# First layer of a two-layer decoder trunk: normalising after the first projection instead of before it

## The chip, the cores and the metric

The kernel runs on one core of a Trainium2 chip. The metric is the device time of one execution in microseconds. The core has a tensor engine (PE, with its weight loads shown as PEld), a vector engine (DVE), a scalar engine (ACT), GpSimd (POOL), and a sync engine (SP) that issues nearly all DMAs. Each engine works off its own queue of instructions and waits at semaphores for the others.

## The reference, cut to what matters

Two layers act on x of 512 rows by 1024 columns, in float32:

```
h = RMSNorm(x) * norm_g              # rstd by row, gain by column
p = h @ w_in                         # 1024 -> 3488 columns
cq, ckv, kr, g_a, c_h, c_b, c_c, g_b, sg_u, sg_v, g_c, mq, mk, mv, g_d = split(p)
o_a = latent attention: q = rmsnorm(rmsnorm(cq) @ w_uq), k and v from rmsnorm(ckv) @ w_ukv, rotary part
o_b = c_b * causal_conv3(c_c * c_h)
o_c = sg_u * (masked 128x128 mix of layernorm(sg_v))
o_d = block attention with q = rmsnorm(mq), k = rmsnorm(mk), v = mv
x   = x + concat(o_a silu(g_a), o_b silu(g_b), o_c silu(g_c), o_d silu(g_d)) @ w_out
```

Since rstd is one number per row of x, p of a row is that number times the row of (x * norm_g) @ w_in. Where p goes into another RMSNorm or LayerNorm, the factor cancels but for the epsilon, which has to be divided by rstd squared, that is, multiplied by the mean square.

## The kernel before, in words

**Precision.** Every matrix is kept as a high part in the fast float32 format of the tensor engine and a low part (the remainder). A product is three matmuls: high by high, high by low, low by high (mm3). High parts are made by a copy on ACT or DVE (split2, split_units), low parts by a subtraction on DVE or POOL (low_half).

**Order of the work.** The order of each engine's instructions is written out by a planner in Python: every step of the kernel is a generator (a "chain") that asks an engine for an instruction with an estimated cost and resumes when the planned clock has come that far. What a chain issues stands in the engine's queue from then on; the queues are worked off in that order on the chip. All instructions of the chains are recorded at one line of a helper (L164 for ACT, DVE and POOL, L194 for PE, L273 for most DMAs), so the profile is read by tile names. A chain made with a later start time (its due time) is recorded later. DMAs on SP are recorded at the moment the planner reaches them, if a buffer is free; the planner assumes that they land some microseconds on.

**The first layer's start.** start() (L1548) loads x in four row tiles of 128x1024 and the weights c0 to c3 of the first projection (416 columns: cq, ckv, kr; two of the eight contraction blocks in each unit). For each row tile square_half (L628) sums the squares on ACT, pre_norm (L632) makes rstd on POOL (xss), multiplies x by rstd and norm_g on DVE (h), transposes it on PE (hT) and splits it (hTh on ACT, hTl on DVE). norm_g is spread to all partitions by two PE matmuls (ng). Warm-up matmuls (warm) that compute nothing fill PE until about 15 us of planned time. The main generator (L1357) then goes through the row tiles one after the other: tok (L1360) runs all eight contraction blocks of one row tile into one accumulator bank (cq). As soon as a row tile is done, low_chain (L717) multiplies by the gains (ct), transposes (cT) and runs the second projections (q, kv).

**What follows.** Units of weights are loaded through two raw buffers (rawS; four early ones through others) and split; three accumulator banks (accS), three banks for scores (sS) and two for transposes (trS) are handed from step to step. After cq come the sq block (sg_v and mq, four row tiles of 24 matmuls), ga0, ga1, the kv block (mk, mv), and the features su0 to gc1, each 24 matmuls of 512 columns; the attention heads run between them. mix_chain (L837) loads and masks the mixing weights (sgw), and issues the mix products (mp) on PE. rope_tables (L481) makes the sine and cosine tables by polynomials, about 60 small operations on rope_scratch that go to DVE or to POOL, whichever the planner finds free, with a pause from 4.7 to 15.5 us.

**Parameters.** load_params (L565) loads the gains and biases with thirteen small DMAs, most of them spread to all partitions (cg_b, gq_b, gk_b, gr_b, lg_b, lb_b, dq_b, dk_b, ...), when the unit ukv has been issued. In it scale() (L586) multiplies gq_b and dq_b by constants on POOL, in layer 0 not before the planned time MIXT = 23 us:

```
        def scale():
            ch = Chain(o, L.par_t)
            yield from ch.pool(G.tensor_scalar, L.gq, L.gq, -(96 ** -0.5), None, op0=ALU.mult)
            yield from ch.pool(G.tensor_scalar, L.dq, L.dq, -0.125, None, op0=ALU.mult)
        o.spawn(scale(), None if L.l else MIXT, 2)
```

**End of a layer.** The output projection is one Strassen step (seven products of half size, banks oz, ox, oy, line L1382), after which the second layer runs the same code, with its rows normalised before the projection.

Of the kernel before, what the change touches and what calls it, by code (L numbers as in the profile page):

```python
# [11 lines left out]
F32 = mybir.dt.float32  # L12
# [26 lines left out]
ROPEB, ROPEV = 400.0, 200.0  # L39
# [113 lines left out]
class Chain:  # L153
    def __init__(self, o, t=None):
        self.o = o
        self.t = o.now if t is None else t
        self.pe_t = None

    def _emit(self, e, cost, f, a, k):
        while self.t > self.o.now + SLACK:  # L160
            yield self.t - SLACK
        self.o.clk[e] = max(self.o.clk[e], self.t, self.o.now) + cost
        self.t = self.o.clk[e] + LAT
        f(*a, **k)  # L164
# [19 lines left out]
    def pe(self, cost, f, *a, **k):  # L184
# [3 lines left out]
        if self.o.now < self.o.fill_until:  # L188
            for _ in range(int((self.o.now - self.o.pe_end) * FILL / 110.0)):
                self.o.fill()  # L190
# [16 lines left out]
def hybrid_trunk(ctx: ExitStack, tc: tile.TileContext, x, positions, norm_g, w_c, w_f, w_t, w_o, mla_q_norm_g,  # L207
# [33 lines left out]
    zzS = Slots(o, 1, lambda name: wk.tile([P, S + 2], F32, tag="zz", name=name))  # L241
# [37 lines left out]
    class Unit:  # L279
        def __init__(self, src, a, b, name):  # L280
            self.src, self.a, self.b, self.name = src, a, b, name
            self.loaded, self.ready, self.wanted = Event(), Event(), False
            self.half, self.landed = [Event(), Event()], [Event(), Event()]
            self.slots = eS if name[:-2] in EARLY else wS
# [84 lines left out]
    def load_units():  # L369
        for u in order:  # L370
            ch = Chain(o)
            u.raw_slots = rawS
            if u.name in ("c2_0", "c3_0") or u.name[:-3] in ZPROD and u.name[-3] == "1":
# [8 lines left out]
            if u.name == "c0_0":  # L382
                for i in range(2):
# [3 lines left out]
                    o.set(u.landed[i], ch.t)  # L387
            else:
# [6 lines left out]
    def split_units(i0, i1):  # L395
        for u in order[i0:i1]:
# [5 lines left out]
            for i in range(2):  # L402
# [9 lines left out]
                if o.clk["V"] + 600.0 < o.clk["A"] and u.idx > 3:  # L412
# [3 lines left out]
                if u.idx < 4:  # L416
                    o.spawn(low_half(u, i, c2, lo, raw, hi), None, LOPRIO)
# [8 lines left out]
    def low_half(u, i, ch, lo, raw, hi):  # L426
        if (u.name, i) in LOPOOL:
# [29 lines left out]
    nhalf = cst.tile([P, 16], F32, name="nhalf")  # L457
# [15 lines left out]
    posf = cst.tile([P, NT], F32, name="posf")  # L473
    inv = cst.tile([P, 16], F32, name="inv")
    nc.scalar.dma_start(junk[0:NT, 0:P].bitcast(I32), dram(positions, 0, [[P, NT], [1, P]]))
    G.tensor_copy(junk[0:NT, P:2 * P], junk[0:NT, 0:P].bitcast(I32))
# [4 lines left out]
    def rope_tables():  # L481
# [9 lines left out]
        def free_engine():  # L491

            while True:
                if ch.t > o.now + SLACK:
                    yield ch.t - SLACK
                if PAUSE[0] < o.now < PAUSE[1]:
                    yield PAUSE[1]
                if o.clk["V"] <= o.now + ROPEV:
                    return True
                if o.clk["G"] <= o.now + SLACK:  # L500
                    return False
                yield o.now + 60.0

        def dv(f, *a, **k):
            if (yield from free_engine()):
# [4 lines left out]
        def stt(out, in0, c, in1, op0, op1):  # L510
            if (yield from free_engine()):
# [53 lines left out]
    def load_params(L):  # L565
# [24 lines left out]
        o.spawn(scale(), None if L.l else MIXT, 2)  # L590

    layers = []
    for l in range(DEPTH):
# [4 lines left out]
        L.xss = [cst.tile([P, 4], F32, name=f"xss{t}_{l}") for t in range(NT)]  # L598
# [12 lines left out]
        L.hT_free, L.p1, L.h_done, L.h = Event(), Event(), [Event(), Event()], {}  # L611
        L.s = {n: [Event() for _ in range(4)] for n in ("t2", "t1", "b22")}
# [11 lines left out]
    def pow_rstd(ch, dst, src, n):  # L624
        return ch.pow(G.tensor_tensor, dst, src, nhalf[:, :n], op=ALU.pow)

# [62 lines left out]


    def low_stats(L, t, a, t0, done):
# [9 lines left out]
        yield from ch.dve(V.tensor_scalar, m[:, 0:2], ssq[:, t, 1:3], 1.0, EPS, op0=ALU.mult, op1=ALU.add)  # L701
        yield from ch.dve(V.tensor_scalar, m[:, 2:4], ssq[:, t, 0:2], EPS, EPS * EPS, op0=ALU.mult, op1=ALU.add)
# [14 lines left out]
    def low_chain(L, t, a, t0):  # L717
        ch = Chain(o, max(t0, L.par_t))
        l = L.l
        done = shared(accS, 2)  # L720
# [30 lines left out]
    def q_chain(L, t, q_ps, t0):  # L751
# [13 lines left out]
        for h in range(4):  # L765
            yield from ch.act(A.activation, junk[:, :96], Q[:, t, h, :], AF.Square, accum_out=m[:, h:h + 1])
# [3 lines left out]
        yield from pow_rstd(ch, m[:, 4:8], m[:, 0:4], 4)  # L770
        for h in range(4):
# [8 lines left out]
    def kv_chain(L, t, kv_ps, t0):  # L780
# [22 lines left out]
        for h in range(4):  # L803
            yield from ch.act(A.activation, junk[:, :64], K[:, t, h, 0:64], AF.Square, accum_out=m[:, h:h + 1])
# [8 lines left out]
    def sv_chain(L, t, a, t0, put):  # L813
# [11 lines left out]
        yield from ch.pool(G.tensor_scalar, mv[:, 1:2], mv[:, 1:2], 1.0, EPS, op0=ALU.mult, op1=ALU.add)  # L825
# [11 lines left out]
    def mix_chain(L):  # L837
# [32 lines left out]
    def gate(ch, a, name):  # L870
        th = yield from t2S.get(ch, f"th_{name}")
        yield from ch.act(A.activation, th, a, AF.Tanh, scale=0.5)
# [55 lines left out]

    def su_chain(j):
        def f(L, a, t0):  # L930
# [3 lines left out]
            accS.put(ch)  # L934
            yield from ch.wait(L.mix_ev)
# [6 lines left out]
            yield from ch.dve(V.tensor_tensor, u, mt, u, op=ALU.mult)  # L942
# [5 lines left out]
    def finish(ch, L, kt, yv, tg):  # L948
        yield from ch.dve(V.scalar_tensor_tensor, yv, in0=yv, scalar=0.5, in1=tg, op0=ALU.mult, op1=ALU.mult)
# [14 lines left out]
    def ch_chain(j):  # L964
        def f(L, a, t0):
# [3 lines left out]
            accS.put(ch)  # L969
            o.set(L.b_ev[j][0], ch.t)  # L970
        return f

    def cc_chain(j):
        def f(L, a, t0):
# [5 lines left out]
            yield from ch.dve(V.tensor_tensor, zz[:, 2:S + 2], a, c, op=ALU.mult)  # L980
# [5 lines left out]
            zzS.put(ch)  # L986
            o.set(L.b_ev[j][1], ch.t)
        return f

    def cb_chain(j):  # L990
        def f(L, a, t0):
            ch = Chain(o, t0)
            yield from ch.wait(L.b_ev[j][1])
            yield from ch.dve(V.tensor_tensor, L.b[j], a, L.b[j], op=ALU.mult)
# [22 lines left out]
    def mqk_chain(nm):  # L1017
        def f(L, t, a, t0, put):
# [12 lines left out]
            for h in range(4):  # L1031
                yield from ch.act(A.activation, junk[:, :64], dst[:, t, h, :], AF.Square, accum_out=m[:, h:h + 1])
            yield from ch.pool(G.tensor_scalar, m[:, 0:4], m[:, 0:4], 1.0 / 64, EPS, op0=ALU.mult, op1=ALU.add)
            yield from pow_rstd(ch, m[:, 4:8], m[:, 0:4], 4)
            for h in range(4):
# [10 lines left out]
    def mv_chain(L, t, a, t0, put):  # L1046
# [6 lines left out]
        yield from split2(ch, mt[:, :, 0:64], mt[:, :, 64:128], a[:, 0:256].rearrange("p (h d) -> p h d", h=4))  # L1053
# [51 lines left out]
    def pv_chain(L, H):  # L1105
# [25 lines left out]
        if h == 3:  # L1131
            v4S.put(ch)
            v4S.put(ch)
        H.ya_left[0] -= 1
# [222 lines left out]
    def main():  # L1357
        m = Chain(o)

        def tok(L, n, width, t, dst, us):  # L1360

            for k in range(KT):
# [3 lines left out]
                if (n, t, L.l) == ("c", 0, 0):  # L1366
                    us[k // 2:] = [(yield from unit(m, f"{n}{k // 2}_{L.l}", k % 2))]
                elif len(us) == k // 2:
# [7 lines left out]
                yield o.now  # L1376

# [4 lines left out]
        def seven(L):  # L1382
# [36 lines left out]
            slot = {"z0": accS, "z1": accS, "x0": accS, "x1": sS, "y0": sS, "y1": sS}  # L1419
            for n in ZPROD:  # L1420
                for i in range(2):
                    b = home.get(n, "y") + str(i)
                    ev = evs[n, i] = Event()
                    if n in ("b11", "t3"):
# [4 lines left out]
                    if (l, n, i) == (DEPTH - 1, "b22", 1):  # L1429
                        ev2 = Event()  # L1430
                        yield from z_out(L, "u", i, a, m.t, ev2, sS.put)
# [6 lines left out]
                    if n == "b11":  # L1438
                        y = bank[f"y{i}"] = yield from sS.get(m, f"oy{i}_{l}")
# [12 lines left out]
        for L in layers:  # L1452
# [8 lines left out]
            for t in L.torder:  # L1461
                a = yield from accS.get(m, f"cq{t}_{l}")
                yield from tok(L, "c", 416, t, a[:, 0:416], us)
                o.spawn(low_chain(L, t, a, o.now + PELAT))
# [7 lines left out]
            for n in SEQ:  # L1472
                if n in TOKS:
                    us = []
                    for t in range(NT):
                        a = yield from accS.get(m, f"{n}{t}_{l}")
# [189 lines left out]
```

## Time and profile before

| what | value |
|---|---|
| median of 3 runs | 499.86 us (498.12 to 500.18) |
| the profiled execution's own time | 499.26 us |
| its span | 497.6 us |
| PE busy | 490.7 us, 99% |
| DVE, ACT, POOL busy | 384.1 (77%), 320.7 (64%), 150.6 us (30%) |
| DMA | 81.98 MB, mean 165 GB/s |

A row of the timeline reads: start in us, duration in us, engine, line, operation, output tile <- input tiles, shapes, count, and in brackets how long the engine sat idle before it and who released it. A row of a group reads: busy us, mean ns of one | idle us before it and what ended that. A row of a window reads: stretch, its length, busy us (and instructions) of PE, PEld, DVE, ACT and POOL, granted clock, DMA share, GB/s. A row of DMA issues ends with the size of one and the median us from issue to landing. Matmul durations overlap, since matmuls are pipelined: the distance from start to start says what one costs. SPq is SP's issuing of DMAs.

### The profile page before, as it was taken

How to read it: one execution, taken by the hardware profiler on the slowest of the kernel's cores; microseconds unless marked ns; L12 is line 12 of the kernel's file. 1: busy time of each engine (PE TensorE's matmuls, PEld its weight loads, DVE VectorE, ACT ScalarE, POOL GpSimd, SP SyncE). 2: the span in 40 equal slices, each digit the busy share in tenths (PEclk: the TensorE clock that was granted, in tenths of full speed). 3: DMA queues.
4: the chain of work that ended last, by engine and by line, in shares of the span. 5: the costliest groups of instructions: out<-in, count | busy, mean ns of one | idle time of the engine just before them, and what ended most of it. 6: DMA issues, size and time to landing. Idle time of an engine off the chain costs nothing.

```text
span 497.6 us, 7823 instructions
## 1 busy us (share of the span) xinstructions
PE 490.7 (99%) x2459; PEld 416.4 (84%) x2459; DVE 384.1 (77%) x998; ACT 320.7 (64%) x938; POOL 150.6 (30%) x310
## 2 busy tenths in 40 slices
PE   8999989999999999999999999999999999999997
PEld 5998878888888888888889987788888888888886
DVE  3887885567797978699898698757888979765992
ACT  5788754557767786667566995557868676524640
POOL 4656785566100000000041478634250010000000
PEclk9999999999999999999999999999999999999999
DMA  8446549472752445587573232576259464475652
GB/s 306 110 144 212 198 100 235 147 156 54 202 139 84 149 148 135 157 315 247 165 258 129 84 125 88 193 191 102 67 191 232 150 154 122 166 258 180 229 171 96
DMA packets 35459, 81.98 MB, mean 165 GB/s; under 512 B 7125, under 2 KB 16857, under 8 KB 35162
## 3 DMA queue, kind: packets, MB, share of 16 engines
q1 hardware_dynamic: 26960, 73.09, 43.1%
q0 software_dynamic: 8448, 8.39, 11.3%
q8 instruction: 19, 0.31, 0.3%
q14 instruction: 22, 0.18, 0.1%
q10 hardware_dynamic: 10, 0.01, 0.0%
HBM read 73.61 MB, written 24.64 MB: 197 GB/s over the span
## 4 chain that ended last, share of the span: by engine, by line
PE 89%; DVE 3%; ACT 3%; POOL 3%; issue 1%; POOLq 0%; DVEq 0%
PE kv L194 10%; PE cq L194 8%; PE oy L194 6%; PE ch L194 4%; PE cc L194 4%; PE gd L194 4%; PE gb L194 4%; PE cb L194 4%; PE gc L194 4%; PE su L194 4%; PE ox L194 4%; PE oz L194 4%; PE sa L194 3%; PE ga L194 2%; PE od L194 2%; PE oa L194 2%
## 5 line engine op out<-in xcount | busy, mean ns | idle before, releaser
L164 ACT ACTIVATE pd<-pd,mnd 128x256 f32<-128x256 f32 (+3 forms) x48 | 26.0, 555 | 1.4 <-DVE mnd L164 1.4
L164 ACT ACTIVATE pha<-pTa 128x512 fp32r<-128x512 f32 (+3 forms) x32 | 13.9, 436 | 20.0 <-PE pTa L194 19.8
L194 PE MATMUL kv<-whi_kv,hTh 128*128 128x512 f32 x64 | 25.9, 405 | 0.0
L164 ACT ACTIVATE pa<-pa,mna 128x256 f32<-128x256 f32 (+3 forms) x46 | 23.9, 537 | 2.7 <-DVE mna L164 2.7
L164 ACT ACTIVATE phd<-pTd 128x512 fp32r<-128x512 f32 (+3 forms) x32 | 13.8, 434 | 17.8 <-PE pTd L194 17.8
L164 DVE TENSOR_TENSOR pla<-pTa,pha 128x512 fp32r<-128x512 f32 (+3 forms) x32 | 15.2, 484 | 12.8 <-ACT pha L164 12.7
L194 PE MATMUL kv<-whi_kv,hTl 128*128 128x512 f32 x64 | 25.0, 391 | 0.0
L194 PE MATMUL kv<-wlo_kv,hTh 128*128 128x512 f32 x64 | 24.9, 390 | 0.0
L194 PE MATMUL cq<-whi_c,hTh 128*128 128x416 f32 x64 | 24.4, 382 | 0.0
L339 POOL DMA_DIRECT2D t<-in_w_o_dram x16 | 17.5, 1097 | 19.9 <-DMA t<-t 19.3
L194 PE MATMUL cq<-whi_c,hTl 128*128 128x416 f32 x64 | 23.0, 360 | 0.0
L194 PE MATMUL cq<-wlo_c,hTh 128*128 128x416 f32 x64 | 22.9, 357 | 0.0
L164 POOL TENSOR_SCALAR xss<-xss 128x1 f32<-128x1 f32 x8 | 3.1, 391 | 61.8 <-ACT jk L164 49.1
L164 ACT ACTIVATE whi_t<-raw_t 128x512 fp32r<-128x512 f32 x31 | 18.2, 621 | 5.7 <-DMA raw_t<-t 5.7
L164 DVE TENSOR_TENSOR wlo_t<-raw_t,whi_t 128x512 fp32r<-128x512 f32 x32 | 21.1, 683 | 0.0
L164 DVE CUSTOM_DVE_ANT_0 pa<-sa,maskb 128x512 f32<-128x512 f32 (+3 forms) x32 | 15.0, 482 | 6.2 <-PE sa L194 3.1
L164 DVE CUSTOM_DVE_ANT_0 pd<-sd,maskb 128x256 f32<-128x256 f32 (+3 forms) x32 | 14.9, 485 | 5.9 <-PE pTd L194 2.8
L194 PE MATMUL sq<-yTh,hTh 128*128 128x512 f32 x48 | 18.9, 393 | 0.0
L194 PE MATMUL sq<-yTh,hTl 128*128 128x512 f32 x48 | 18.7, 390 | 0.0
L194 PE MATMUL sq<-yTl,hTh 128*128 128x512 f32 x48 | 18.7, 389 | 0.0
L164 DVE TENSOR_TENSOR pld<-pTd,phd 128x512 fp32r<-128x512 f32 (+3 forms) x32 | 15.3, 482 | 3.2 <-ACT phd L164 3.1
L164 ACT ACTIVATE whi_b<-raw_b 128x512 fp32r<-128x512 f32 x24 | 14.5, 622 | 4.2 <-DMA raw_b<-in_w_o_dram 4.2
(379 smaller groups left out, 1856.0 us busy)
## 6 DMA issues: line engine op xcount, KB each, us to landing
t<-in_w_o_dram POOLq DMA_DIRECT2D x16, 512.0 KB, 6.7
raw_t<-t SPq DMA_DIRECT2D x16, 512.0 KB, 4.2
raw_b<-in_w_o_dram SPq DMA_DIRECT2D x12, 512.0 KB, 4.4
raw_sq<-in_w_t_dram SPq DMA_DIRECT2D x8, 512.0 KB, 3.6
t<-in_w_o_dram SPq DMA_DIRECT2D x8, 512.0 KB, 4.4
raw_kv<-in_w_t_dram SPq DMA_DIRECT2D x8, 512.0 KB, 3.5
t<-t SPq DMA_DIRECT2D x8, 512.0 KB, 5.5
ys<-ysc SPq DMA_DIRECT2D x14, 256.0 KB, 4.8
```

What stands on the lines that cost most here:

```text
L164: f(*a, **k)
L194: f(*a, **k)
L339: nc.gpsimd.dma_start(z_src(l, n, j), quad(l, b, j), accum_op=ALU.add, max_dma_last_dim=1024)
```

## The change

In layer 0 the rows are no longer normalised ahead of the projection.

- x is loaded by column blocks (two of 128 columns, then three of 256, for all 512 rows), interleaved with the units c0 to c3. Each block of 128 columns is transposed on PE as it is (xT); norm_g, now a column per block (gcol), is applied in the split (x_parts).
- c_first runs the first projection with the contraction outside: for each column block the 12 products of the four row tiles, in the order high by high, low weights, low x. Four banks (three accS, one sS) are open at once. The last two blocks go by row tile. The low halves of c0 both, and the first halves of c1 to c3, are made on POOL; the high parts on DVE.
- x_stats sums the squares of x in 16 pieces on ACT; rstd (r) and the scaled epsilons are made for all rows at once. They are applied to results: in v of the block attention, in the gates (a DVE multiply by the row rh, half of rstd spread over partitions by two PE matmuls, x_row), and on POOL in by_rstd for su, ch and the convolution.
- head_sums may square on POOL and add on DVE instead of four squares on ACT, in both layers.
- The rope table starts on DVE (five operations) and goes on on POOL, without the pause.
- scale() has no due time of its own any more; users of gq_b and dq_b wait for it in the plan (g_ev). uq and ukv are loaded through the two h buffers, so that they and the parameters need not wait for a raw buffer.
- mix_chain of layer 0 is due at 42 us instead of 23, and in both layers its products are issued 2 us after the last row it needs.
- In the Strassen step the banks change places (z1 and x0 in sS, y0 and y1 in accS), and the bank x1 is taken when the last head of the block attention is done.
- Fill matmuls are fewer and different.

```diff
-NWARM, FILL, FILLEND = 3, 0.6, 15000.0
-ROPET, PAUSE, MIXT = 3900.0, (4700.0, 15500.0), 23000.0
-LOPOOL = (("c0_0", 1), ("c1_0", 1), ("c2_0", 1), ("c3_0", 1))
+NWARM, FILL, FILLEND = 4, 0.7, 15000.0
+MIXT, MIXLAG, ROWT = 42000.0, 2000.0, 38000.0
+KSPLIT, SQPOOL, LOVEC = 6, 200.0, 1
...
-            if u.name in ("c2_0", "c3_0") or u.name[:-3] in ZPROD and u.name[-3] == "1":
+            if u.name in ("uq_0", "ukv_0"):
+                u.raw_slots = hS
+                u.raw = yield from hS.get(ch, f"raw_{u.name}")
+            elif u.name in ("c2_0", "c3_0") or u.name[:-3] in ZPROD and u.name[-3] == "1":
...
-        if (u.name, i) in LOPOOL:
+        if i == 0 or u.idx < LOVEC:
             yield from ch.pool(G.tensor_tensor, lo, raw, hi.bitcast(F32), op=ALU.subtract)
...
             yield from ch.pool(G.tensor_scalar, L.dq, L.dq, -0.125, None, op0=ALU.mult)
-        o.spawn(scale(), None if L.l else MIXT, 2)
+            o.set(L.g_ev, ch.t)
+        o.spawn(scale(), None, 2)
...
+    def x_parts(k, tp, t0):
+        L, ch = layers[0], Chain(o, t0)
...
+        yield from ch.act(A.activation, hi, tp, AF.Copy, scale=g)
+        o.set(xhi[k], ch.t)
+        yield from ch.dve(V.scalar_tensor_tensor, lo, in0=tp, scalar=g, in1=hi.bitcast(F32),
+                          op0=ALU.mult, op1=ALU.subtract)
...
+        yield max(o.now, ch.t) + MIXLAG
         L.mix = (yield from hS.get(ch, f"mix{l}")).rearrange("p (n g d) -> p n g d", n=NT, g=4)
...
+        if name[-1] == "0":
+            yield from ch.wait(rh_ev)
+            yield from ch.dve(V.tensor_tensor, th, a, rh_box[0][:, 0:S], op=ALU.mult)
...
+            yield from x_transpose(0)
+            for k in range(KSPLIT):
+                for i in range(3):
+                    yield from ready(k, i)
+                    for t in range(NT):
+                        yield from part(k, t, i)
+                    if i == 0 or i == 1 and k + 1 == KSPLIT:
+                        yield from x_transpose(k + 1 + i)
...
-            slot = {"z0": accS, "z1": accS, "x0": accS, "x1": sS, "y0": sS, "y1": sS}
+            slot = {"z0": accS, "z1": sS, "x0": sS, "x1": sS, "y0": accS, "y1": accS}
...
+                    if b == "x1":
+                        yield from m.wait(L.s_done)
```

More of the change, by code (lines that the diff above doesn't have):

```diff
@@ L282, in __init__ @@
             self.loaded, self.ready, self.wanted = Event(), Event(), False
-            self.half, self.landed = [Event(), Event()], [Event(), Event()]
+            self.half, self.high, self.landed = ([Event(), Event()] for _ in range(3))
             self.slots = eS if name[:-2] in EARLY else wS
@@ L770, in q_chain @@
         yield from pow_rstd(ch, m[:, 4:8], m[:, 0:4], 4)
+        yield from ch.wait(L.g_ev)
         for h in range(4):
@@ L927, in s_chain, with by_rstd @@
         o.set(L.s["b22"][kk], ch.t)
+    def by_rstd(ch, z, n):
+        yield from ch.wait(rh_ev)
+        for _ in range(n):
+            yield from ch.pool(G.tensor_tensor, z, z, rh_box[0][:, 0:S], op=ALU.mult)
+        rh_put(ch)
     def su_chain(j):
@@ L1545, in hybrid_trunk @@
     L0 = layers[0]
-    L0.x0, L0.xh = [Event() for _ in range(NT)], [Event(), Event()]
     def start():
```

332 lines of the change are left out of this document (232 added, 100 removed).

## The prediction

> **What bounds the kernel now.** I read the page first (busy shares, chain), then the waits of the tensor engine (PE), then its timeline at the start, then the windows around its few gaps.
>
> ```profile
> span 497.6 us, 7823 instructions
> PE 490.7 (99%) x2459; PEld 416.4 (84%) x2459; DVE 384.1 (77%) x998; ACT 320.7 (64%) x938; POOL 150.6 (30%) x310
> PE 89%; DVE 3%; ACT 3%; POOL 3%; issue 1%; POOLq 0%; DVEq 0%
> ...
> PE mp L194 <- ACT vnh L164: 2.1, 2, 1.3
> ...
> 69.00:71.00 2.00, 0.69 (x4) 0.27 (x2) 1.90 (x5) 1.76 (x8) 1.39 (x3) 1.00 0.99 151
> 71.00:73.00 2.00, 1.89 (x11) 1.52 (x12) 1.06 (x6) 0.78 (x2) 1.92 (x2) 1.00 1.12 195
> 310.00:320.00 10.00, 9.12 (x45) 7.32 (x44) 6.92 (x21) 5.49 (x15) 6.24 (x18) 1.00 0.56 210
> ```
>
> PE is the bound from end to end. The only gaps behind the start and ahead of the tail are those at the spatial mix (mp), where PE waits for the split rows vn: 1.31 + 0.11 + 0.88 = 2.3 us not busy in these three windows. Neither PE's useful instructions nor their shapes change, so the change is worth what it does to the start and to gaps. The start:
>
> ```profile
> 1.26 2.93 PE L1557 MATMUL warm<-ones 128*128 128x256 f32 x6 [1.26 <-DVE ones L164]
> 9.90 1.06 PE L194 MATMUL hT<-ident,h 128*128 128x128 f32 x4
> 10.62 0.69 PE L194 MATMUL cq<-whi_c,hTh 128*128 128x416 f32 x1
> ...
> 12.57 0.55 PE L194 MATMUL cq<-wlo_c,hTh 128*128 128x416 f32 x1
> 12.92 0.55 PE L194 MATMUL cq<-whi_c,hTl 128*128 128x416 f32 x1
> ...
> 13.98 0.43 PE L194 MATMUL cq<-whi_c,hTh 128*128 128x416 f32 x1
> ...
> 14.63 0.35 PE L194 MATMUL cq<-whi_c,hTh 128*128 128x416 f32 x1
> 14.82 0.35 PE L194 MATMUL cq<-wlo_c,hTh 128*128 128x416 f32 x1
> ...
> 16.20 0.60 PE L194 MATMUL hT<-ident,h 128*128 128x128 f32 x4
> 16.55 0.44 PE L194 MATMUL cq<-whi_c,hTh 128*128 128x416 f32 x1
> ```
>
> Most of the 14 us is warm-up (fill) matmuls, which compute nothing. A cq matmul starts every 0.35 us at 12.6 us and every 0.19 us from 14.6 us on; four transposes take 0.35. By 13.98 us PE has done six cq matmuls and eight transposes, 6 x 0.19 + 2 x 0.35 = 1.84 us of full-speed work: the start loses 13.98 - 1.84 = **12.1 us**. That is the sum's reference.
>
> **The start after the change.** Column block 0 of x and the first half of c0 are enough for the first products, so on paper PE starts early. But the order of instructions of the changed program shows what stands in the way. GpSimd (POOL) now has, ahead of everything of the projection: the scaling of gq_b, the scaling of dq_b, then both low halves of c0 (wlo_c), then the rope table. Before, the two scalings came after all low halves and all four rstd. They moved because scale() is no longer held to 23 us, and the parameter loads, no longer kept back by a raw slot, are recorded at once, so that the planned landing lies at 4 us. On PE the ninth product (wlo_c of column block 0) is queued right behind eight transposes and four cq matmuls. So: dq_b lands -> POOL scales it -> POOL makes wlo_c -> PE goes on. Whether POOL really stands behind such a load, and what the steps cost:
>
> ```profile
> 6.91 1.06 POOL L164 TENSOR_TENSOR wlo_c<-raw_c,whi_c 128x416 fp32r<-128x416 f32 x1 [0.50 <-ACT whi_c L164]
> ...
> 24.67 0.46 POOL L164 TENSOR_SCALAR gq_b<-gq_b 128x96 f32<-128x96 f32 x1
> 25.21 0.37 POOL L164 TENSOR_SCALAR dq_b<-dq_b 128x64 f32<-128x64 f32 x1
> ...
> 196.24 0.47 POOL L164 TENSOR_SCALAR gq_b<-gq_b 128x96 f32<-128x96 f32 x1 [22.16 <-DMA gq_b<-in_mla_q_g_dram]
> 199.04 0.37 POOL L164 TENSOR_SCALAR dq_b<-dq_b 128x64 f32<-128x64 f32 x1 [2.33 <-DMA dq_b<-in_moba_q_g_dram]
> ```
>
> In layer 1 POOL sits idle for gq_b and then again for dq_b, in its order; there nothing urgent is queued behind. In layer 0 of the changed kernel wlo_c is.
>
> When does dq_b land? It is the eighth of the parameter loads in SP's queue, and in the listing each load waits for the one eight places ahead of it: dq_b for raw_ukv, which is behind all of x, c and raw_uq.
>
> ```profile
> 12.00:13.00 1.00, 1.00 (x5) 0.95 (x5) 1.00 (x3) 1.00 (x4) 0.63 (x2) 1.00 1.00 404
> 13.00:14.00 1.00, 1.00 (x8) 0.88 (x6) 1.00 (x2) 1.00 (x3) 1.00 (x2) 1.00 0.42 166
> ...
> 13.81 0.33 SPq L273 DMA_DIRECT2D raw_ukv<-in_mla_w_ukv_dram  x1
> 17.51 0.43 SPq L550 DMA_DIRECT2D dq_b<-in_moba_q_g_dram  x1
> 195.19 0.33 SPq L550 DMA_DIRECT2D dq_b<-in_moba_q_g_dram  x1
> ...
> raw_uq<-in_mla_w_uq_dram SPq DMA_DIRECT2D x1, 384.0 KB, 6.2
> raw_ukv<-in_mla_w_ukv_dram SPq DMA_DIRECT2D x1, 256.0 KB, 2.7
> dq_b<-in_moba_q_g_dram SPq DMA_DIRECT2D x1, 32.0 KB, 5.7
> ```
>
> Before, x, c and raw_uq (4 MB) keep the queue full until about 13.4 us (404 GB/s, then 166 in the window in which they end). Changed, raw_ukv's 262 kB follow without a pause: 262/404 = 0.65 us, so 14.1, landing at about 14.4 us. dq_b is then issued at 14.5. From issue to landing it took 5.7 us at the start of before; in layer 1, 199.04 - 195.19 = 3.85 us; a quiet load like raw_ukv 2.7 us. From raw_ukv's landing (13.81 + 2.7 = 16.5) to dq_b's (23.2) it was 6.7 us. That bounds dq_b's landing to 17.1 (14.4 + 2.7) and 21.1 us (14.4 + 6.7); I take 14.5 + 5.7 = **20.2 us**, its own row with the same small loads ahead of it. x now comes in runs of 512 bytes and 1 KB, for which no row gives a rate; the 0.9 us up to the upper bound have to cover a slower x.
>
> Then 0.37 for dq_b, 1.06 for wlo_c, 0.2 for the hand-overs (24.67 + 0.46 to 25.21 is 0.08 each): PE goes on at 21.8 us. It has by then done four cq matmuls and eight transposes, 1.46 us. After more than ten idle microseconds I take it to start at the slow spacing: from 10.62 to 13.98 us it cost 3.36 x (1 - 0.19/0.35) = 1.5 us; bounds are 0 and half of the whole slow stretch of before (1.26 to 13.98), some 5.8 us; I take 1.5, measured on the same matmuls. Loss 21.8 - 1.46 + 1.5 = 21.9 us, against 12.1: **+9.8 us**. The Trainium skill (TensorE: Matmul & The Clock Gate, What's actually happening) has the array at half clock by default, at full after a window of about 3.4 us of activity, and back at half after one idle window. The profile's granted clock says 1.00 throughout, while the spacing halves at 13.98, so the spacing decides; by that page an unlucky window would cost up to 3.4 us (6.8 us at half rate) instead of 1.5, and the sum would be 1.9 us higher.
>
> **The other parts, each against its cover.** The second wlo_c of c0 stands behind five rope operations and itself costs 1.06 to 1.28; POOL needs 3.3 us for them, PE has twelve slow products, 4.2 us, so no wait; the later low halves have longer.
>
> ```profile
> L164 POOL TENSOR_SCALAR rope_scratch<-rope_scratch 128x64 f32<-128x64 f32 x23 | 10.2, 443 | 2.2 <-DVE rope_scratch L164 0.9
> L164 POOL TENSOR_TENSOR rope_scratch<-rope_scratch 128x64 f32<-128x64 f32 x11 | 6.1, 555 | 0.9
> L164 POOL TENSOR_TENSOR wlo_c<-raw_c,whi_c 128x416 fp32r<-128x416 f32 x4 | 5.1, 1284 | 0.9 <-ACT whi_c L164 0.9
> L164 POOL TENSOR_TENSOR mq<-mq,nhalf 128x4 f32<-128x4 f32 x4 | 4.1, 1036 | 7.8 <-DVE mq L164 4.6 <-DVE bmv L164 2.4 <-DVE ms L164 0.8
> L164 POOL TENSOR_TENSOR ms<-ms,nhalf 128x2 f32<-128x2 f32 x4 | 2.8, 709 | 1.7 <-DVE ms L164 1.7
> L164 DVE SCALAR_TENSOR_TENSOR h<-x,xss,ng 128x512 f32<-128x512 f32 x8 | 5.9, 740 | 0.5 <-PE ng L1563 0.5
> L164 ACT ACTIVATE whi_c<-raw_c 128x416 fp32r<-128x416 f32 x8 | 3.8, 545 | 0.4 <-DMA raw_c<-in_w_c_dram 0.4
> 41.19 3.44 PE sq L194 x15
> ```
>
> Normalising x goes (8 x 0.74 us of DVE); the high halves of c come to DVE (8 at the 0.55 us that ACT took); both lie under PE, as do the sums of squares of x by 16 pieces on ACT. rstd on the results adds on DVE eight 128x512 multiplies at the gates (8 x 0.74 = 5.9 us) and on POOL eight 128x512 multiplies (1.28 x 512/416 = 1.6 each, 12.6 us), spread over the 24-product features, 24 x 0.23 = 5.5 us of PE each with three accumulator banks; if that cover is gone, one late gate holds a bank for its 0.74 us. The row of rstd adds two PE matmuls of 512, 0.45 us. Squares by head move from ACT to POOL in part. Mix issued later: its loads go behind two more units on SP and its products behind 18 kv products; I take both mp waits as gone, **-2.3 us**, bounds 0 and -2.3 (what is late next is the gate of the first feature that needs the mix, 24 products on). Bank x1 waits until the last head is done: in the listing both layers have 48 or more feature products between the last head product and the first Strassen product, so nothing; without that cover it would be up to one 24-product block, 5.5 us.
>
> Sum against the profiled execution, 499.26 us: 499.26 + 9.8 + 0.45 - 2.3 = 507.2. The median of the runs before, 499.86, lies 0.6 above it, so I forecast **507.8 us**.
>
> **The rivals.** *Faster: the load does not hold POOL.* If gq_b and dq_b are in place when POOL comes to them, wlo_c of block 0 is done at 8.0 us as before (6.91 + 1.06), the start loses 8.1 - 1.46 + 1.5 = 8.1 us, and the time is 499.86 - 4.0 + 0.45 - 2.3 = 494.0. It decides where dq_b lands before about 12 us: 9.8 - 1.85 = 7.95 us earlier than 20.2. For it: x and c land early enough. Against: raw_ukv, for which dq_b waits, lands after 14 us.
>
> *Nearly the same: loads land early and PE starts fast.* dq_b at 17.1 and no slow stretch: 507.8 - 3.1 - 1.5 = 503.2; with a microsecond or two won elsewhere 501 to 503.
>
> *Slower still: POOL becomes the bound of the first stage.* Between wlo_c and the release of the first sq bank POOL has 33 + 25 rope operations (14.6 + 13.9), five wlo_c (6.4), the powers (about 6.7, from 0.71 to 1.04 each) and three squares (3.5): 45 us from 20.6, so 66 us. PE comes to the fourth sq block at 21.8 + 1.5 + 92 x 0.19 + 72 x 0.23 + about 10 for the small products, 67 us. The margin is 1 to 2 us; a POOL 10% slower than these rows gives a wait of 3 to 4 us: 511. The Trainium skill (SBUF — State Buffer, Who interferes with whom) lets VectorE copies and GpSimd lock each other out of a shared port for whole instructions. The wlo_c rows, 1.06 us at first and 1.28 in the mean, agree with something of the kind; the copies of c's high halves now on DVE would add to it, which is part of this rival's chance.
>
> **How the numbers follow.** POOL held, margin kept: 0.62 (503 to 510). POOL bound as well: 0.20 (510 to 513.5). Loads early: 0.10 (499 to 503). Not held: 0.08 (493 to 497). The range leaves out the last two and the end of the second: 502.8 to 513. 0.5% is what a measurement can tell, 497.4 to 502.4: faster 0.08, same 0.05 (half of the third), slower 0.87.
>
> **What would show it.** Right: POOL idle from about 4 us to 20 us, released by the DMA of gq_b and then dq_b; PE idle from 8 or 9 us to about 22 us at a cq product with wlo_c, released by POOL; cq products 0.35 us apart right after; no mp wait. Wrong: wlo_c before 12 us, or PE waits later in layer 0 for POOL or for banks, or in the last blocks of a layer.

## The result and the profile after

The changed kernel takes 515.45 us (median of 4 runs, 514.28 to 516.3), the kernel before 499.77 beside it: a ratio of 1.032 (95% interval 1.029 to 1.035), 15.7 us slower. Forecast were 507.8 us and a range of 502.8 to 513.0: the sign is right, the size is not. The profiled spans differ by the same amount, 513.3 against 497.6 us.

The page of the changed kernel (span, busy shares, chain, the costliest group):

```profile
span 513.3 us, 7783 instructions
PE 488.4 (95%) x2449; PEld 414.2 (81%) x2449; DVE 400.1 (78%) x1004; ACT 307.9 (60%) x869; POOL 178.3 (35%) x354
...
PE 72%; POOL 10%; DVE 8%; DMA 4%; ACT 2%; issue 2%; SPq 1%; POOLq 0%
...
L196 PE MATMUL cq<-wlo_c,hTh 128*128 128x416 f32 x64 | 20.8, 372 | 13.6 <-POOL wlo_c L166 13.6
```

PE was busy for 99% of the span and is at 95%; POOL now holds 10% of the chain. Where PE waits in the changed kernel (total us, times, longest):

```profile
PE cq L196 <- POOL wlo_c L166: 13.6, 1, 13.6
PE kv L196 <- ACT mix L166: 1.7, 1, 1.7
PE ga L196 <- DVE vn L166: 1.5, 2, 1.1
...
PE rrow L196 <- DVE rdl L166: 0.9, 1, 0.9
...
PE pTd L196 <- DVE pld L166: 0.6, 1, 0.6
PE t0a L196 <- DVE Q L166: 0.5, 1, 0.5
```

Left out are waits of the `warm` matmuls ahead of the first product. The first line is the forecast one. The other five, 5.2 us together, are new; the two mp waits of before (2.1 us) are gone. The timelines of SP's queue, POOL and ACT in the changed kernel show who holds whom:

```profile
16.61 0.33 SPq L559 DMA_DIRECT2D dq_b<-in_moba_q_g_dram  x1
...
17.39 0.49 POOL L166 TENSOR_SCALAR gq_b<-gq_b 128x96 f32<-128x96 f32 x1 [14.33 <-DMA gq_b<-in_mla_q_g_dram]
21.06 0.38 POOL L166 TENSOR_SCALAR dq_b<-dq_b 128x64 f32<-128x64 f32 x1 [3.17 <-DMA dq_b<-in_moba_q_g_dram]
21.39 1.07 POOL L166 TENSOR_TENSOR wlo_c<-raw_c,whi_c 128x416 fp32r<-128x416 f32 x1
...
96.76 0.63 ACT L166 ACTIVATE whi_su<-raw_su 128x512 fp32r<-128x512 f32 x1 [3.19 <-DMA raw_su<-in_w_f_dram]
97.30 0.46 ACT L166 ACTIVATE mix<-mp,sgb 128x256 f32<-128x256 f32 x1
```

And PE itself, at the start and where the late waits are:

```profile
22.51 1.76 PE L196 MATMUL cq<-wlo_c,hTh 128*128 128x416 f32 x4 [13.58 <-POOL wlo_c L166]
24.07 1.59 PE L196 MATMUL cq<-whi_c,hTl 128*128 128x416 f32 x4
...
26.88 1.00 PE L196 MATMUL cq<-wlo_c,hTh 128*128 128x416 f32 x4
...
75.75 0.47 PE L196 MATMUL ga<-hTh,whi_ga 128*128 128x512 f32 x1 [0.45 <-DVE vn L166]
79.16 0.50 PE L196 MATMUL rrow<-rdl,ones 128*128 128x512 f32 x1 [0.86 <-DVE rdl L166]
84.12 0.47 PE L196 MATMUL ga<-hTh,whi_ga 128*128 128x512 f32 x1 [1.06 <-DVE vn L166]
98.69 0.50 PE L196 MATMUL kv<-whi_kv,hTh 128*128 128x512 f32 x1 [1.65 <-ACT mix L166]
```

Up to 26.88 us PE has done 16 cq matmuls and 12 transposes, 16 x 0.19 + 3 x 0.35 = 4.1 us: the start loses 22.8 us, 10.7 more than before. The first ga comes at 75.75 us, where it came at 63.93: 11.8 us late. So 3.9 us of the 15.7 arise behind the first ga.

### The profile page after: what moved, and what is told of

It reads as the page before. It is cut to its first block, busy times and chain, and to the rows that moved or that the text cites. A ratio compares the mean times of both kernels' runs of the same rounds, so it can differ in the third digit from the quotient of the medians.

```text
span 513.3 us, 7783 instructions
## 1 busy us (share of the span) xinstructions
PE 488.4 (95%) x2449; PEld 414.2 (81%) x2449; DVE 400.1 (78%) x1004; ACT 307.9 (60%) x869; POOL 178.3 (35%) x354
## 4 chain that ended last, share of the span: by engine, by line
PE 72%; POOL 10%; DVE 8%; DMA 4%; ACT 2%; issue 2%; SPq 1%; POOLq 0%
PE kv L196 7%; PE oy L196 6%; POOL rope_scratch L166 5%; PE gb L196 4%; PE gd L196 4%; PE cb L196 4%; PE su L196 4%; PE gc L196 4%; PE ox L196 4%; PE oz L196 4%; PE ch L196 4%; PE cq L196 4%; PE cc L196 3%; PE sa L196 3%; PE oa L196 2%
## 5 line engine op out<-in xcount | busy, mean ns | idle before, releaser
L196 PE MATMUL cq<-wlo_c,hTh 128*128 128x416 f32 x64 | 20.8, 372 | 13.6 <-POOL wlo_c L166 13.6
L166 POOL TENSOR_TENSOR chs<-chs,rh 128x512 f32<-128x512 f32 x6 | 8.3, 1390 | 51.1 <-ACT chs L166 32.5
L166 ACT ACTIVATE pa<-pa,mna 128x256 f32<-128x256 f32 (+3 forms) x41 | 21.7, 539 | 6.9 <-DVE mna L166 6.6
L196 PEld LDWEIGHTS cq<-wlo_c,hTh 128*128 128x128 f32 x64 | 12.1, 198 | 14.1 <-POOL wlo_c L166 14.0
L166 DVE TENSOR_TENSOR wlo_t<-raw_t,whi_t 128x512 fp32r<-128x512 f32 x32 | 21.8, 707 | 1.0 <-ACT whi_t L166 1.0
L196 PE MATMUL cq<-whi_c,hTh 128*128 128x416 f32 x64 | 21.6, 386 | 0.9 <-ACT hTh L166 0.9
L166 DVE SCALAR_TENSOR_TENSOR hTl<-xT,pg,hTh 128x512 fp32r<-128x512 f32 x8 | 6.0, 746 | 20.9 <-ACT hTh L166 20.9
L196 PE MATMUL cq<-whi_c,hTl 128*128 128x416 f32 x64 | 20.3, 365 | 0.0
```

## The experiments

Every edit makes the planner order what follows anew, so each reading below goes by the kernel's own trace. The kernel before, run beside them, took 498.6 to 499.4 us (medians of five batches).

**1. The hold.** Is it the place of the scalings behind late loads? Two edits take the cause away in two ways. First, the scalings are moved behind wlo_c:

```diff
-        o.spawn(scale(), None, 2)
+        o.spawn(scale(), None if L.l else 22000.0, 2)
```

> The changed kernel with one edit: the two scalings of gq_b and dq_b are recorded at 22 us in layer 0, so that on GpSimd they stand behind every low half of c (rows 46 and 49 of its queue) instead of ahead of them. Theory (GpSimd stands in order behind the late dq_b, and the tensor engine's ninth product behind wlo_c): wlo_c of block 0 no longer waits for a load, the tensor engine goes on at about 8.1 us instead of 22.5, a difference of 14.4 us; 515.4 - 14.4 = 501, 499 to 504, with the later waits (vn, rdl, mix behind whi_su) still there. Rival (GpSimd is the bound of the first stage, the hold only brings the wait forward): the start gets shorter, but the equal work from the first ga on keeps its lateness, and the time stays above 510.

Measured: 500.74 us (ratio to before 1.0036, 1.0024 to 1.0048). Second, the order stays and the two loads come first:

```diff
...
+        L0.gq = bcast(mla_q_g, 0, 96, "gq_b", nc.scalar)
+        L0.dq = bcast(moba_q_g, 0, 64, "dq_b", nc.scalar)
...
```

> The changed kernel with the order on GpSimd left as it is (both scalings ahead of wlo_c), but gq_b and dq_b of layer 0 loaded first of all, through ScalarE's queue. Theory: only the landing of the two loads matters, not the scalings (0.49 + 0.38 us in the trace); dq_b lands before about 7 us, the tensor engine goes on at 8 to 9 us, and the time is about 1 us above that of the kernel with the late scalings: 501 to 503. Rival (the place in the queue is what costs, or the extra load delays x and c): above 508.

Measured: 503.72 us (1.010, 1.007 to 1.013), just above the 501 to 503 of its theory. The start of both, POOL and PE, late scalings first:

```profile
5.12 1.06 POOL L166 TENSOR_TENSOR wlo_c<-raw_c,whi_c 128x416 fp32r<-128x416 f32 x1 [2.05 <-DVE whi_c L166]
8.64 1.73 PE L196 MATMUL cq<-wlo_c,hTh 128*128 128x416 f32 x4
```

```profile
8.52 1.08 POOL L166 TENSOR_TENSOR wlo_c<-raw_c,whi_c 128x416 fp32r<-128x416 f32 x1
9.65 1.64 PE L196 MATMUL cq<-wlo_c,hTh 128*128 128x416 f32 x4
```

The hold is the cause of 14.7 us of the 15.7 (of 14.1 when each kernel is set against the kernel before that ran beside it), and it is the loads' landing that makes it. But the second number says more than the first. PE goes on only 1.0 us later with the early loads than with the late scalings, POOL's first wlo_c starts 3.4 us later, and the time is 3.0 us longer. The time follows POOL. Over the three kernels wlo_c at 5.12, 8.52 and 21.39 us goes with 500.7, 503.7 and 515.4 us: 0.88 and 0.91 us per us.

**2. The slow pace after the hold.** Fills, which compute nothing, ahead of the waiting product; first 100, then 55:

```diff
+                    if k == 0 and i == 1:
+                        for _ in range(100):
+                            o.fill()
```

> The changed kernel with 100 matmuls on ones, which compute nothing, ahead of the waiting ninth product, so that the tensor engine is busy while GpSimd waits for dq_b. Theory of the prediction (after more than ten idle microseconds it goes on at half pace and that costs 1.74 us from 22.51 to 26.88): the cq products follow at 0.19 us at once, 515.4 - 1.7 = 513.7, if the fills end before 22.5 us. Rival (the pace after the wait has another cause, such as operands that come late): cq products still 0.35 us apart, time 515 to 516.

> The changed kernel with 55 instead of 100 fills ahead of the waiting ninth product; by the pace of the longer fill (22.8 us for 100) they end near 21.7 us, just ahead of wlo_c. Theory (the slow pace after the idle wait costs 1.74 us): the cq products follow at 0.19 to 0.25 us from the first one on, and the time is 515.4 - 1.7 = 513.7. Rival (the pace has another cause): cq products 0.35 us apart again and 515 to 516.

The 100 ran until 31.7 us, 9.15 us past the place where PE had gone on; the time was 522.54 us and tells nothing of the pace. The 55 ended in time: 515.97 us. PE with the 55 fills:

```profile
21.63 1.02 PE L196 MATMUL cq<-wlo_c,hTh 128*128 128x416 f32 x4
22.48 0.92 PE L196 MATMUL cq<-whi_c,hTl 128*128 128x416 f32 x4
...
24.00 0.60 PE L196 MATMUL xT<-ident,x 128*128 128x128 f32 x4
...
75.86 0.47 PE L196 MATMUL ga<-hTh,whi_ga 128*128 128x512 f32 x1 [0.43 <-DVE vn L166]
```

The pace is full from the first product on, and the second set of transposes comes 2.5 us earlier (24.00 against 26.52). Of that, 0.9 us is not the fills' doing: dq_b landed earlier in this run and released POOL at 20.17 instead of 21.06 us. The other 1.6 us are the pace. Nothing of either is left at the first ga, which starts at 75.86 as it did at 75.75, released by vn. From dq_b to its first work for vn (a scaling of bmv) POOL works without a gap in both kernels, for 41.1 us in the changed kernel and 42.1 with the fills; and VectorE, which makes vn, waits longer for POOL on the way, at krt. Changed kernel, then with the fills:

```profile
DVE krt L166 <- POOL ms L166: 2.9, 4, 1.1
```

```profile
DVE krt L166 <- POOL ms L166: 4.7, 4, 2.8
```

Both theories expected the wrong thing: the slow pace is as large as supposed, and its removal alone gave nothing that four runs can show (515.1 to 518.3 us).

**3. Is GpSimd the bound behind it?** A dose of work on POOL in the kernel with the late scalings:

```diff
+            if L.l == 0:
+                for _ in range(6):
+                    G.tensor_scalar(maskb[:, 0:256], maskb[:, 0:256], 1.0, None, op0=ALU.mult)
```

> The kernel with the late scalings, and behind the scaling of dq_b six multiplications by 1.0 on GpSimd (128x256, some 0.7 us each, 4 to 5 us in all; the values stay as they are). They stand ahead of the rstd of the rows and of nearly all of GpSimd's powers. Theory now (from the hold on, GpSimd is the bound of the first stage, and the time follows its start: first wlo_c at 5.12, 8.52 and 21.39 us went with 500.7, 503.7 and 515.4 us, 0.9 us per us): 500.7 + 4 = 504 to 505.5. Rival (GpSimd has slack, and the tensor engine's own waits set the time): 500 to 501.5.

Measured: 505.46 us, as its theory said (504 to 505.5), 4.7 more than the 500.74 without, for 6.1 us of dose:

```profile
28.96 6.10 POOL L601 TENSOR_SCALAR maskb<-maskb 128x256 f32<-128x256 f32 x6
```

```profile
PE ga L196 <- DVE vn L166: 1.6, 2, 1.3
PE sq L196 <- DVE wlo_sq L166: 1.5, 1, 1.5
PE rrow L196 <- DVE rdl L166: 1.5, 1, 1.5
```

POOL has at most 1.4 us of slack there; without the dose its trace shows only two gaps behind that place up to 89 us, of 0.34 and 0.68 us.

The list names VectorE for vn and rdl. What VectorE itself waits for is on POOL's timeline. In the changed kernel the mean and variance of the second row tile (bmv) are ready on VectorE at 69.0 us; POOL scales them and raises them to a power, and only then can VectorE make vn:

```profile
71.38 0.75 POOL L166 TENSOR_SCALAR bmv<-bmv,xv 128x1 f32<-128x1 f32 x1
...
74.04 0.60 POOL L166 TENSOR_TENSOR bmv<-bmv,nhalf 128x1 f32<-128x1 f32 x1
```

```profile
75.13 0.47 DVE L166 SCALAR_TENSOR_TENSOR vn<-sq,bmv,lg_b 128x256 f32<-128x256 f32 x1
```

Of the 6.1 us from 69.0 to 75.13, 5.6 are POOL's, with two powers and other short work ahead of bmv in its queue. The last rdl, at 78.77, follows a wait of 0.90 us of VectorE for POOL's mk.

Then relief, in the changed kernel. Squares off POOL (SQPOOL = 1e9):

> The changed kernel with the squares by head kept off GpSimd (three instructions, about 3.5 us by their rows). Theory (GpSimd, having idled 17 us for the two loads, is late in the first stage, and the waits for vn and rdl on the tensor engine, 1.5 + 0.9 us, are its lateness): the two waits lose up to 2.4 us, time 513 to 514.5. Rival (vn and rdl wait for VectorE or ScalarE, which the squares now load more): 515 to 517, waits as long or longer.

514.4 us, 1 us less than the changed kernel; the waits for vn and rdl fall from 2.4 to 1.3 us, but new ones for Q, whose scaling factors come from POOL as well, take 3.7 us in a profiled run that was 3 us longer than the others. That is not enough to decide anything. All of the rope table off POOL:

```diff
-ROPEB, ROPEV, ROPES = 400.0, 5, 1500.0
+ROPEB, ROPEV, ROPES = 400.0, 100, 1500.0
```

> The changed kernel with all of the rope table on VectorE (which idles during the hold) instead of all but five operations on GpSimd, some 24 us of GpSimd's work. The wait for wlo_c behind dq_b stays. Theory (GpSimd bound): the waits for vn, rdl and the mix behind it, 1.5 + 0.9 + 1.7 us, go as far as they are GpSimd's lateness; 511 to 513.5, and the first ga starts a few us earlier than 75.8. Rival (these waits come from elsewhere, or VectorE is then late): 515 to 517.

513.62 us, 1.8 less by the medians, just above the 511 to 513.5 of its theory. Four runs, 512.1 to 515.4 us, don't make that clear of noise (1.031 against 1.032 times the kernel before). The trace says more: the waits for vn and rdl are gone. But the first ga comes at 76.07 us, no earlier than without the edit, with no wait of PE right ahead of it: there PE's own late start sets it. And both at once, the rope table off POOL and the 55 fills:

> The changed kernel with both the 55 fills ahead of the waiting product (they alone gave 516.0, no gain) and the rope table on VectorE (it alone gave 513.6). Theory (the tensor engine's start and GpSimd's work bind together; the 2.5 us that the tensor engine gains at the start pay only where GpSimd is relieved): 511 to 512. Rival (the slow start was hidden or made up elsewhere, whatever GpSimd does): 513 to 514.5.

510.52 us (1.0234, 1.0216 to 1.0251), 4.9 us less than the changed kernel and clear of noise; the theory's 511 to 512 is just missed. The first ga comes at 74.41 us. The stretch from 60 to 80 us (width; busy us of PE, PEld, DVE, ACT and POOL with their counts; granted clock, DMA share, GB/s), in the order changed kernel, rope table on DVE, both:

```profile
60.00:80.00 20.00, 18.70 (x82) 14.86 (x81) 18.93 (x64) 12.32 (x60) 19.31 (x31) 1.00 0.46 171
```

```profile
60.00:80.00 20.00, 20.00 (x90) 16.57 (x89) 17.79 (x70) 13.86 (x66) 14.03 (x18) 1.00 0.49 171
```

```profile
60.00:80.00 20.00, 20.00 (x89) 16.24 (x87) 17.80 (x70) 13.42 (x65) 13.74 (x17) 1.00 0.44 161
```

In the changed kernel POOL is busy for 19.3 of 20 us and VectorE for 18.9; relieved of the rope table, POOL is busy for 14.0, VectorE has more instructions to do there (70 against 64), and PE has no gap. So it is POOL, not the amount of VectorE's work, that made PE wait. Fills alone give nothing, both edits 4.9 us: the fills pay only once POOL is relieved (513.62 to 510.52 by the medians; 1.7 us in the profiled spans, 510.4 to 508.7). After the hold PE's late, slow start and POOL's late work run side by side, and the later of the two sets the time. They are not terms of a sum. What the relief alone is worth, four runs leave open: between 0.3 and 1.8 us by the times, 2.9 by the spans of the two profiles.

**4. What the earlier start buys.** With the late scalings the first ga starts at 63.76 us, no earlier than before (63.93), though PE goes on at 8.64. A load stands in ACT's queue there:

```profile
25.04 0.63 ACT L166 ACTIVATE yTh<-raw_sq 128x512 fp32r<-128x512 f32 x1 [3.07 <-DMA raw_sq<-in_w_t_dram]
...
26.49 0.67 ACT L166 ACTIVATE hTh<-xT,pg 128x512 fp32r<-128x512 f32 x1
...
27.21 0.46 PE L196 MATMUL cq<-whi_c,hTh 128*128 128x416 f32 x1 [2.01 <-ACT hTh L166]
```

Two holds take such loads out of ACT's way, the first alone, then both:

```diff
+            if u.name == "sq0_0":
+                yield from ch.wait(xhi[7])
+            if u.name == "su0_0":
+                yield from ch.wait(layers[0].mix_ev)
```

> The kernel with the late scalings, and the split of the first sq unit recorded behind the eighth column block's transposes, so that on ScalarE hTh of blocks 6 and 7 does not stand behind the late load raw_sq. Theory (2.0 us of wait at 27.2 us and then ten cq products at 0.35 instead of 0.19 us, 1.6 us): 500.7 - 3.6 = 497.1. Rival (the sq products become late by what the cq products gain): 499 to 501.

> The same kernel with one more hold: the split of the first su unit is recorded behind the mix, so that on ScalarE the mix does not stand behind the late load raw_su. Theory (a wait of 1.4 us for the mix goes): 1.4 us below the kernel with hTh first, 495.7 if that one gives 497.1. Rival (su's own products then wait): no difference between the two kernels.

504.65 and 500.75 us: the first theory fell, and of the second the direction held and the size did not (3.9 us below the first hold alone instead of 1.4). The wait and the slow pace at 27 us are gone in both, but the planner, with other clocks, puts the powers for mq and mk ahead of those for bmv on POOL; the first bmv comes at 54.5 and 55.3 us instead of 48.6 (VectorE has it ready at 52.3 and 52.6 instead of 46.8, so POOL's order is only a part of this), and PE waits for vn (3.2 and 3.5 us) and in the first also for Q (3.0). With the rope table off POOL as well it is no better. On the late scalings alone and on both holds:

> The kernel with the late scalings and all of the rope table on VectorE. Theory (GpSimd bound): vn comes earlier, the wait for vn (0.3 us) goes, but ScalarE still holds hTh behind raw_sq (3.6 us with the slow pace after it); 497 to 500. Rival (GpSimd has slack here): 500.7 or, with VectorE later, above.

> The kernel with the late scalings, hTh ahead of the sq split, the mix ahead of the su split, and all of the rope table on VectorE. Theory (with GpSimd relieved, the earlier products at last pay): below the kernel with late scalings and rope on VectorE by 3 to 5 us, 494 to 497, thus below the kernel before. Rival (another engine, VectorE at 10.0 of 10 us from 50 us on, is the next bound): 499 to 501, no gain.

500.95 us (1.0056, 1.0033 to 1.0078; ten runs from 499.2 to 504.2, no gain clear of noise) and 503.42 us, above its theory and its rival. So with the late scalings the rope table is no longer what holds POOL's results back. In the second kernel POOL is busy for only 4.4 us from 40 to 50 us, then waits for VectorE:

```profile
50.91 2.40 POOL L166 TENSOR_TENSOR mk<-mk,nhalf 128x4 f32<-128x4 f32 x2 [4.45 <-DVE mk L166]
```

VectorE is busy for 9.7 of the next 10 us; bmv, ready on it at 52.5 us, is scaled by POOL only at 56.15, behind powers for mk and mq. Whether VectorE's amount of work or the order on both engines is the limit there, no run separates. What would come of the two holds with POOL's order kept was not tried.

**5. The mix.** The term was -2.3 us. The lag alone, in the kernel before:

```diff
+        yield max(o.now, ch.t) + 2000.0
         L.mix = (yield from hS.get(ch, f"mix{l}")).rearrange("p (n g d) -> p n g d", n=NT, g=4)
```

> The kernel before with the lag of 2 us ahead of the mix and nothing else. Theory of the prediction's term (both mp waits go): 499.8 - 2.3 = 497.5 at best. Rival (the lag alone moves the wait elsewhere, or leaves the products in the same place in the tensor engine's queue): 499 to 501, the mp rows still in the chain of waits or a wait of another tile in their place.

497.21 us (0.9967, 0.9954 to 0.9980): 2.0 us less, and the only version here that beats the kernel before. Its waits:

```profile
PE mp L194 <- DVE th_ga L164: 1.2, 2, 0.7
```

The mp waits fall from 2.1 to 1.2 us, not to zero; the first ga of this profile is already 1.6 us earlier than before's, ahead of any mix, so at most 1 us of the gain is shown to be the mix's. The other way round, the mix of the changed kernel as before (MIXT 23000, MIXLAG 0):

> The changed kernel with the mix issued as in the kernel before (its loads at 23 us, no lag), all else as changed. Theory of the prediction's term (issuing it later is worth 2.3 us): 517.7. Theory now (in the changed kernel the wait for the mix behind raw_su, 1.65 us, stands in place of the mp waits): within 1 us of 515.4, with mp waits back and the wait for the mix at kv gone.

517.49 us (515.8 to 518.7), 2.0 more than the changed kernel: near the size that the prediction gave, with 0.6 of it in the profiled run in the hold itself (PE goes on at 23.09 instead of 22.51). But not for its reason:

```profile
79.99 0.47 PE L196 MATMUL ga<-hTh,whi_ga 128*128 128x512 f32 x1 [2.96 <-DVE Q L166]
...
101.16 0.51 PE L196 MATMUL kv<-whi_kv,hTh 128*128 128x512 f32 x1 [1.57 <-ACT mix L166]
```

No mp wait comes back, the wait for the mix stays, and the loss stands at the first ga, where PE waits for Q: POOL's order again (the first bmv starts at 65.8 instead of 62.2 us, with two powers for mq right ahead of it). With the late scalings, where POOL is earlier (PE waits 0.3 us for vn), the same edit does nothing:

> The kernel with the late scalings and the mix issued as in the kernel before. Theory now (the lag is worth nothing here, the two waits replace each other): 500 to 501.5. Theory of the prediction's term: 503.

500.24 against 500.74 us, as the theory said. And with the split of su behind the mix there:

> The kernel with the late scalings, and the split of the first su unit recorded behind the mix (the hold on the sq split is left out), so that on ScalarE the mix does not stand behind the late load raw_su. Theory (the wait of 1.4 us for the mix goes, nothing else moves): 500.7 - 1.4 = 499.3. Rival (what the split of su loses, its products wait for): 500.5 to 501.5.

500.06 us (1.0015, 1.0004 to 1.0025), 0.7 less than without by the medians and 1.0 by the ratios, between the 1.4 of the theory and the nothing of its rival; the wait for the mix is gone from the list, and waits for Q and pld (0.8 and 0.6 us) stand in its place. This is the nearest that the changed kernel came to the kernel before.

**6. The release of the scaling alone.** In the kernel before:

```diff
-        o.spawn(scale(), None if L.l else MIXT, 2)
+        o.spawn(scale(), None, 2)
```

> The kernel before with the scaling of gq_b and dq_b no longer held, and nothing else. In the order of its instructions the two scalings then stand behind all four wlo_c on GpSimd, because there the loads of the parameters themselves are recorded late (behind raw slots). Theory (it takes both parts, the release and the loads recorded at once): no change, 498.5 to 500.5. Rival (the release alone holds GpSimd and delays what follows, the rstd and the rope table): 502 or more.

503.11 us (1.0083, 1.0065 to 1.0100): the theory fell and the rival holds. POOL and PE:

```profile
23.41 0.40 POOL L164 TENSOR_SCALAR dq_b<-dq_b 128x64 f32<-128x64 f32 x1 [3.09 <-DMA dq_b<-in_moba_q_g_dram]
...
24.30 0.57 POOL L164 TENSOR_TENSOR xss<-xss,nhalf 128x1 f32<-128x1 f32 x1
```

```profile
21.25 0.63 PE L194 MATMUL hT<-ident,h 128*128 128x128 f32 x4 [1.48 <-DVE h L164]
27.43 1.12 PE L194 MATMUL hT<-ident,h 128*128 128x128 f32 x8 [2.36 <-DVE hTl L164]
```

There no wlo_c stands behind the loads, but the rstd of the last row tiles does: 1.5 + 2.4 = 3.8 us of wait on PE, and 3.95 us in the time.

## Why the prediction was wrong in size

- **The hold: right.** POOL idle for gq_b and dq_b in turn, PE idle at a wlo_c product, both as foretold; dq_b released POOL at 21.06 us (forecast 20.2, bounds 17.1 to 21.1), PE went on at 22.51 (21.8). The load was issued at 16.61 instead of 14.5, the step "dq_b is then issued at 14.5" being wrong by 2.1 us, and took 4.4 us instead of 5.7. Removing the hold gave 14.7 us.
- **The slow pace: right in size, 1.74 against 1.5 us, wrong as a term.** Its removal gave nothing alone, and 1.7 us in the traces (3.1 by the medians) once POOL was relieved.
- **The start in all: +10.7 against +9.8.** This mis-sizing accounts for 0.9 of the 7.6 us between forecast and result.
- **The step that failed: the margin of 1 to 2 us between POOL and PE, which the main case counted only to the release of the first sq bank.** There it held: vn read that bank at 66.04 us (forecast 66), and PE came to the fourth sq block, which needs it, at 69.70 (forecast 67) without a wait. But POOL's queue goes on without a gap, and the sum has no term of POOL's for the second and the third bank. From the end of the first bmv power (64.84) to that of the second (74.64) POOL needs 9.8 us, while PE does a row tile of sq in 5.4 (64.27 to 69.70). So PE waits for vn at the first ga (0.45 us) and again at 84.12 (1.06), and for rdl (0.86): 2.4 us that the main case put at nothing. "POOL becomes the bound of the first stage" had been set apart as a rival that would take the place of the main case, at 510 to 513.5 us; it came together with the main case, behind the place that was counted, and 515.45 lies beyond it. Relief with the fills gave 4.9 us. The 10% slower POOL of that rival, blamed on a shared port, isn't there in wlo_c in the changed kernel (1.07 to 1.09 us against 1.28 in the mean before); with the 55 fills three of them took 1.21 to 1.45 us. Whether a port is behind that isn't shown.
- **The mix, -2.3: its first half right, its second wrong.** The mp waits went (2.1 us). "What is late next" was named as the gate of the first feature that needs the mix; in truth it was kv, which waits for the mp bank, since whi_su stood ahead of the mix on ACT, behind a late load: +1.65. Further waits, pTd and t0a, add 1.1 us.
- **The sum by the traces:** start +10.7; 1.1 more by the first ga (0.45 of it the wait for vn); rdl 0.86, the second vn 1.06, mix 1.65, pTd 0.62, t0a 0.48, the two rrow matmuls 0.45, less the mp waits 2.1: 10.7 + 1.1 + 3.0 = 14.8 of 15.7. The rest, 0.9 us, is in steps that I can't name. Of the 7.6 us between forecast and result, vn and rdl are 2.4, the mix 1.9, pTd and t0a 1.1 and the start 0.9; some 1.4 have no name.
- **The rival "not held" (494.0) was wrong in its price.** Not held, the kernel takes 500.7: the saving of 4 us at the start was gone by the first ga. It was priced by PE's start alone, as the main case was.
- **Bank x1, the features' rstd, the gates: nothing, as foretold.** No wait above 0.2 us names them in the changed kernel. The gates have little to spare: with the rope table on VectorE a wait for th_ga at kv appears, of 0.9 to 1.2 us in three kernels.

## What to carry to other kernels

An instruction that waits for a load stops everything behind it on its engine, however urgent: before releasing or moving one, list what its engine and the queues behind it do next, and put short work on late loads behind the critical work (here worth 14.7 us, and in the kernel before, where it looked harmless, 3.95). When such a hold idles two engines at once, their delays are not added but compared: count the other engine's queue to the end of the stage, not to the first release. Measure each engine's lateness from the end of the hold, and test with one edit for each and one for both. And a list of waits names only the last releaser: vn was put down to VectorE, whose own waits led on to GpSimd, and the time followed GpSimd.

## What the runs showed of the hardware

The pace of PE fell after a much shorter pause than I had thought of, and there the granted clock shows it. With the late scalings, after the wait of 2.01 us at 27.21 us, the cq products are 0.35 us apart until 30.96; the windows from 28 to 30 and from 31 to 32 us of that run:

```profile
28.00:30.00 2.00, 1.98 (x6) 1.89 (x7) 1.82 (x6) 1.57 (x5) 1.49 (x4) 0.50 0.75 242
...
31.00:32.00 1.00, 1.00 (x7) 1.00 (x6) 0.96 (x3) 0.46 (x3) 0.83 (x3) 1.00 0.60 98
```

The granted clock fell to 0.50 as well after single waits of 2.56 us (hTh first) and 2.32 us (late scalings, the mix as before), and to 0.62 in the window from 28 to 30 us after one of 1.68 us (the mix first). But the length of the wait alone doesn't decide: after 2.96 us for Q (the changed kernel with the mix as before, at 79.99), after 3.57 us (both holds with the rope table on VectorE, at 60.63) and after the 1.65 us for the mix in the changed kernel the matmuls are 0.23 us apart at once. What else it depends on isn't shown. After the hold of 13.6 us the granted clock reads 1.00 while the products are 0.39 us apart, so there the column doesn't tell. The Trainium skill (TensorE: Matmul & The Clock Gate, What's actually happening) puts the fall to half rate at one idle window of about 3.4 us; here falls followed single waits of 1.7 to 2.6 us and one of 3.57 us was not followed, and the measurement decides. That the pace stays low for about 3 us agrees with its window.
